# Query tiles of an attention in four places by turns, two of them shared with the quarters that the zs products load

## The chip, the cores and the metric

The kernel runs on one core of a Trainium2 chip. The core has five engines that run beside each other, each with an instruction queue of its own that is worked off in order: TensorE (PE, matrix products, with its weight loads shown apart as PEld), VectorE (DVE), ScalarE (ACT), GpSimd (POOL) and SyncE (SP, which here only issues DMAs). On-chip memory is divided into 128 partitions; matrix products land in eight banks of a second, smaller memory. The metric is the device time of one execution in microseconds.

## What is computed

One layer of a streaming encoder: x of 1024 tokens by 1024 channels, normalised, projected to queries, keys, values and five gates; a windowed attention (16 query heads, 2 key heads, 64 channels a head, keys of the own 64-token chunk and the two before it, one learned sink a head) and a spatial gating run side by side, are gated, projected, summed, projected again and added to x.

```python
proj = rmsnorm(x, norm_g) @ w_in
q, k, v, za, u, vs, zs, gm = jnp.split(proj, IN_SPLITS, axis=-1)
a = window_sink_attention(partial_rope(q), partial_rope(k), v, sinks)
a = (a * silu(za)) @ w_att_out
sgo = chunked_spatial_gating(gelu(u), gelu(vs), sg_w, sg_b, ln_g, ln_b)
sgo = (sgo * silu(zs)) @ w_sg_out
ga, gs = split(sigmoid(gm + b_merge))
x = x + (ga * a + gs * sgo) @ w_o
out = rmsnorm(x, final_g)
```

## The kernel before

Every float32 product is made of three products of rounded parts (a high and a low part of each factor), and every pair of 128-row weight blocks is multiplied in the manner of Strassen, with seven products of 12 matmuls instead of eight. `gemm_pair` (L327) does one pair: the products b11, t1, t2, b21, t3, b22 and t4 in this order, b11, t2, t3 and t4 adding onto one bank (`acc`), t1 and b22 onto another (`t5`), b21 into a third. ScalarE copies the bank after b11 into x11 (L336), after t1 into x22 (L340) and after t2 into x12 (L343); VectorE later adds to these tiles (L348, L353, L357), and each finished quarter goes to `finish`, the fourth in a further x tile. So a pair takes four x tiles, and the pool has five. Weights come through SP into `wr` tiles (L186), are split by ScalarE and VectorE (L151, L152), and the products read the parts.

After the products for q, the code runs four pairs for zs (m = 0, 2, 4, 6) through `zs_pair` (L936): the four quarters of a pair are kept in their x tiles, passed through Silu (L940), multiplied by quarters of the spatial gating's result (L943), which `get` loads from the scratch array s1_dr (L186), and stored to s_dr (L425). The profile shows both arrays as s_dr. For m = 0 the loaded quarters lie in the five `rot` places of an earlier pool; for m = 2, 4 and 6 in two places of the tag `g` in the pool `attention`. A quarter fills [128, 512] float32. Eight pairs for the gates gs and ga follow.

The attention runs beside the zs pairs of m = 2, 4, 6 and those of gs and ga. It has 32 steps: two key heads, eight token tiles of 128, two parities (which half of the query heads). `attention` (L1045) is a generator: in iteration n it emits the transposes of the weights of step n - 2 (L1015), then the scores and the softmax of step n (L975 to L1006), then the load of the query tile of step n + 2 (L923), then the product with the values of step n - 2 (L1034). `gemm_pair` calls a hook after each of its seven products, and each hook emits one or more of these parts: one in the zs pairs, 75/56 on average in the later ones. Seven hooks in the pair of m = 2 thus reach the scores of step 3, those of m = 4 the values of step 3 and the scores of step 5, those of m = 6 the scores of step 7 and the weights of step 6.

`query_stage` (L917) allocates the query tile, [128, 4, 128], which has the size of a quarter, and loads it with two DMAs; for every even step `key_stage` (L906) loads keys (L909) and values (L914) ahead of it. Query tiles have two places, tag `q` in the pool `ahead`, so that the tile of step n replaces that of step n - 2. `first_loads` issues those of steps 0 and 1 during the zs pair of m = 0.

The memory places are handed out when the instruction order is made, before the run: a tile that asks for a place of a tag gets one as soon as the last reader of a tile before it is listed, and its first writer then waits for that reader. The order on each engine's queue is listed in the same pass. It follows the order of the code where instructions are ready, and moves later ones ahead where earlier ones are not; on the chip each queue then keeps that order.

Of the kernel before, what the change touches and what calls it, by code (L numbers as in the profile page):

```python
# [25 lines left out]
F32R = mybir.dt.float32r  # L26
# [5 lines left out]
P = 128  # L32
# [22 lines left out]
def hybrid_tile(  # L55
# [25 lines left out]
    def nm(s):  # L81
        count[0] += 1
        return f"{s}_{count[0]}"
# [4 lines left out]
    def mtile(shape, dt, tag, bufs, pool=None):  # L88
        return (pool or main).tile(shape, dt, name=nm(tag), tag=tag, bufs=bufs)
# [621 lines left out]
    pool = stage.enter_context(tc.tile_pool(name="mixing", bufs=1))  # L711
# [90 lines left out]
    aheads = ahead.enter_context(tc.tile_pool(name="ahead", bufs=1))  # L802
    stage = ExitStack()
    pool = stage.enter_context(tc.tile_pool(name="queries", bufs=1))
# [94 lines left out]
    steps = [(g, t, par) for g in range(2) for t in range(NT) for par in range(2)]  # L899
# [5 lines left out]
    def key_stage(g, t):  # L905

        k0 = 0 if t else P
        kt = mtile([P, 2, 256], F32R, "k", 2, aheads)
        nc.sync.dma_start(  # L909
            kt[:, :, k0:].bitcast(F32), k_dr[:, 2 * g : 2 * g + 2, (t - 1) * P + k0 : (t + 1) * P]  # L910
        )
        vt = mtile([P, 2, 3 * HD], F32R, "v", 2, aheads)
        for j in key_tiles(t):
            nc.sync.dma_start(vt[:, j, :].bitcast(F32), v_dr[t - 1 + j, :, g, :])  # L914
        keys[g, t] = [kt, vt, None]

    def query_stage(g, t, par):  # L917
        if par == 0:
            key_stage(g, t)
        qt = mtile([P, 4, P], F32R, "q", 2, aheads)  # L920
        for j in range(2):
            rows = q_hl[j].rearrange("(c r d) t -> r d c t", r=2, d=HD)[par]
            nc.sync.dma_start(  # L923
                qt[j * HD : (j + 1) * HD].bitcast(F32), rows[:, 4 * g : 4 * g + 4, t * P : (t + 1) * P]
            )
        return qt
# [3 lines left out]
    def first_loads():  # L930
        for n in range(2):
            qT.append(query_stage(*steps[n]))
            yield
# [18 lines left out]
    pool = stage.enter_context(tc.tile_pool(name="attention", bufs=1))  # L952
# [92 lines left out]
    def attention():  # L1045

        held = []
        for n, step in enumerate(steps):
            if n >= 2:
                pT = weight_stage(*steps[n - 2], held.pop(0))  # L1050
                yield
            held.append(softmax_stage(*step, qT.pop(0)))
            if n + 2 < len(steps):
                qT.append(query_stage(*steps[n + 2]))
            yield
            if n >= 2:
                value_stage(*steps[n - 2], pT)
                yield
        for n in (-2, -1):
            pT = weight_stage(*steps[n], held.pop(0))  # L1060
            yield
            value_stage(*steps[n], pT)
            yield
# [25 lines left out]
    pool = stage.enter_context(tc.tile_pool(name="later", bufs=1))  # L1089
# [239 lines left out]
    for p in range(4):  # L1329
        n, t, acc, x11 = N_PAIRS + p, T_ORDER[p], accs[p], firsts[p]  # L1330
# [169 lines left out]
```

## Time and profile before

| | us |
|---|---|
| three runs | 965.46, 961.13, 967.64 |
| median | 965.46 |
| the profiled execution | 962.22 |
| its span, first to last instruction | 960.4 |
| TensorE without work in the span | 32.7 |
| the attention's scores, first to last | 328 to 630 |

The profile is of one execution. A row of the timeline gives the start, the length, the engine, the line, the operation and the names of what is written and read; in brackets stands how long the engine was idle before it and what ended that. A row of the waits gives who waited, for whom, how long in all, how often, and the longest. In the rows SPq is SP's queue of DMAs: its length is the time to issue, not to land.

### The profile page before, as it was taken

The page shows a single profiled execution, that of the slowest core. Times are in us where ns is not written, and L with a number is a line of the kernel's source. Part 1 is how long each engine was busy: PE and PEld are TensorE (multiplying, and loading weights), DVE is VectorE, ACT ScalarE, POOL GpSimd, SP SyncE. Part 2 cuts the span into 40 slices and gives each one's busy share as a digit, 9 for nine tenths or more (in the row PEclk, how much of TensorE's full clock was granted, in tenths as well). Part 3 has the DMA queues.
Part 4 walks back from the last instruction along what each step waited for, and adds up shares of the span by engine and source line. Part 5 has one row for each costly group of instructions (what it writes and reads, how often), then busy time and mean ns, then how long its engine had stood idle before and what let it go on. Part 6 is the DMA issues. An engine that isn't in the chain of part 4 may idle for free.

```text
span 960.4 us, 13432 instructions
## 1 busy us (share of the span) xinstructions
PE 927.7 (97%) x4452; PEld 767.6 (80%) x4452; DVE 692.0 (72%) x1321; ACT 558.1 (58%) x1061; POOL 120.5 (13%) x201
## 2 busy tenths in 40 slices
PE   6999999999999989999999998999999999999996
PEld 5888888888888878788878877888887887787885
DVE  6744677666675778788878876755589489569995
ACT  7864333333444489977767675754475465457443
POOL 0202212221000001211101111000110011210011
PEclk9999999999999999999999998999999999999999
DMA  7343767888669657876566694849758757979632
GB/s 277 121 128 129 212 211 187 184 156 191 214 231 319 201 184 209 228 197 158 156 210 218 210 229 122 215 145 321 287 197 309 286 191 246 272 190 306 219 122 87
DMA packets 126549, 198.64 MB, mean 207 GB/s; under 512 B 11408, under 2 KB 59280, under 8 KB 126480
## 3 DMA queue, kind: packets, MB, share of 16 engines
q1 hardware_dynamic: 108864, 149.28, 46.8%
q0 software_dynamic: 17472, 48.24, 21.2%
q8 instruction: 35, 0.57, 0.3%
q14 instruction: 34, 0.28, 0.1%
q10 hardware_dynamic: 144, 0.26, 0.1%
HBM read 141.65 MB, written 85.46 MB: 236 GB/s over the span
## 4 chain that ended last, share of the span: by engine, by line
PE 45%; DVE 9%; ACT 4%; DMA 3%; issue 3%; SPq 0%; DVEq 0%; ACTq 0%
PE ps_mm L318 19%; PE ps_o L318 15%; PE ps_sc L975 3%; PE ps_o L1034 3%; PE ps_tp L1015 2%; DMA wr<-in_w_dram 2%; DVE wl L152 2%; PE ps_tp L318 2%; PE ps_sc L318 2%; DVE bq L172 1%; DMA wr<-y_dr 1%; ACT pr L987 1%; ACT wh L151 1%; DMA g<-s_dr 0%; DVE T_t3l L152 0%
## 5 line engine op out<-in xcount | busy, mean ns | idle before, releaser
L151 ACT CAST wh<-s 128x1024 fp32r<-128x1024 f32 (+1 forms) x76 | 76.0, 1002 | 96.0 <-PE ps_mm L318 43.4
L151 ACT CAST wh<-wr 128x1024 fp32r<-128x1024 f32 (+1 forms) x78 | 64.5, 828 | 73.8 <-PE ps_mm L318 33.2
L152 DVE TENSOR_TENSOR wl<-wr,wh 128x1024 fp32r<-128x1024 f32 (+1 forms) x78 | 74.0, 950 | 43.7 <-ACT wh L151 42.8
L152 DVE TENSOR_TENSOR wl<-s,wh 128x1024 fp32r<-128x1024 f32 (+1 forms) x76 | 88.6, 1167 | 14.9 <-ACT wh L151 13.4
L987 ACT ACTIVATE pr<-pr,sm 128x256 f32<-128x256 f32 (+1 forms) x128 | 62.5, 490 | 23.6 <-DVE sm L977 23.3
L977 DVE CUSTOM_DVE_ANT_0 pr<-ps_sc,mask,nsink_sb 128x256 f32<-128x256 f32 (+1 forms) x128 | 56.3, 463 | 13.8 <-PE ps_sc L975 13.2
L318 PE MATMUL ps_o<-T_t1h,wh 128*128 128x512 f32 x144 | 57.3, 398 | 0.9 <-ACT wh L151 0.9
L318 PE MATMUL ps_o<-T_b22h,wh 128*128 128x512 f32 x144 | 57.2, 397 | 0.0
L318 PE MATMUL ps_mm<-T_b11h,wl 128*128 128x512 f32 x136 | 54.3, 399 | 2.4 <-DVE wl L152 2.4
L975 PEld LDWEIGHTS ps_sc<-k,q 128*128 128x128 f32 x256 | 40.4, 189 | 20.2 <-DVE sm L977 16.3
L318 PE MATMUL ps_o<-T_t1h,wl 128*128 128x512 f32 x144 | 56.3, 391 | 0.1
L975 PE MATMUL ps_sc<-k,q 128*128 128x256 f32 (+1 forms) x256 | 48.2, 294 | 8.5 <-DVE sm L977 8.4
L318 PE MATMUL ps_o<-T_b22h,wl 128*128 128x512 f32 x144 | 56.4, 392 | 0.0
L318 PE MATMUL ps_o<-T_b22l,wh 128*128 128x512 f32 x144 | 56.3, 391 | 0.0
L318 PE MATMUL ps_o<-T_t1l,wh 128*128 128x512 f32 x144 | 56.2, 390 | 0.0
L318 PE MATMUL ps_mm<-T_t4h,wh 128*128 128x512 f32 x136 | 54.1, 398 | 2.0 <-DVE x L353 2.0
L318 PE MATMUL ps_mm<-T_b11h,wh 128*128 128x512 f32 x136 | 54.9, 404 | 0.3 <-ACT wh L151 0.3
L318 PE MATMUL ps_mm<-T_b11l,wh 128*128 128x512 f32 x136 | 54.0, 397 | 0.0
L318 PE MATMUL ps_mm<-T_t3h,wh 128*128 128x512 f32 x136 | 53.7, 395 | 0.0
L318 PE MATMUL ps_mm<-T_t2h,wh 128*128 128x512 f32 x136 | 53.5, 393 | 0.1
L318 PE MATMUL ps_mm<-T_t4h,wl 128*128 128x512 f32 x136 | 53.2, 391 | 0.0
L318 PE MATMUL ps_mm<-T_t3h,wl 128*128 128x512 f32 x136 | 53.2, 391 | 0.0
(360 smaller groups left out, 2548.8 us busy)
## 6 DMA issues: line engine op xcount, KB each, us to landing
wr<-in_w_dram SPq DMA_DIRECT2D x82, 256.0 KB
sums<-in_w_dram POOLq DMA_DIRECT2D x20, 512.0 KB, 5.4
s<-sums SPq DMA_DIRECT2D x20, 512.0 KB
s_dr<-x SPq DMA_DIRECT2D x32, 256.0 KB
q_hl<-qhl SPq DMA_DIRECT2D x16, 512.0 KB
q<-q_hl SPq DMA_DIRECT2D x64, 128.0 KB
wr<-in_w_dram SPq DMA_DIRECT2D x14, 512.0 KB
y_dr<-x POOLq DMA_DIRECT2D x28, 256.0 KB, 5.5
```

Of the source, the lines that this page charges most:

```text
L151: nc.scalar.copy(hi, src)
L152: nc.vector.tensor_sub(lo, src, hi.bitcast(F32))
L172: op(dst[:, i : i + 2, :], a[:, i : i + 2, :], c[:, i : i + 2, :])
L318: nc.tensor.matmul(acc, lt, rt, start=fresh and k == 0 and n == 0, stop=k == 3 and n == 2, skip_group_check=True,)
L975: nc.tensor.matmul(sc[:, js], qt[:, i, :], kt[:, f, k0:], start=f == 0, stop=f == 1)
L977: nc.vector.tensor_tensor_reduce(pr[:, i, k0:], sc[:, js], mask[:, k0:], 1.0, nsink_sb[:, h : h + 1], op0=ALU.add, op1=ALU.min, accum_out= ...
L987: nc.scalar.activation(pr[:, i, k0:], pr[:, i, k0:], AF.Exp, bias=nmax[:, i : i + 1], scale=-1.0, accum_out=sums[:, i : i + 1],)
L1015: nc.tensor.transpose(pt[:, i * P : (i + 1) * P], pr[:, i, kt * P : (kt + 1) * P], ident[:])
L1034: nc.tensor.matmul(po[:], vv, parts[kt][:, n, :], start=kt == tiles[0] and n == 0, stop=kt == 1 and n == 1)
```

## The change

The query tiles of steps n with n % 4 equal to 0 or 1 keep the two places of the tag `q`. Those with n % 4 equal to 2 or 3 take the two places of the tag `g` in the pool that is open when the load is emitted, which is `attention`: the same two places that `zs_pair` uses for the quarters of s1_dr with m = 2, 4 and 6. Nothing else is changed; the loads, their sizes and the place in the code where they are emitted stay.

```diff
     def query_stage(g, t, par):
         if par == 0:
             key_stage(g, t)
-        qt = mtile([P, 4, P], F32R, "q", 2, aheads)
+
+        n = steps.index((g, t, par))
+        qt = mtile([P, 4, P], F32R, "q", 2, aheads) if n % 4 < 2 else mtile([P, 4, P], F32R, "g", 2, pool)
         for j in range(2):
             rows = q_hl[j].rearrange("(c r d) t -> r d c t", r=2, d=HD)[par]
             nc.sync.dma_start(
```

## The prediction

> **What bounds the kernel now.** First the page's busy times, then the table of stretches, cut where the attention runs beside the matrix products.
>
> ```profile
> span 960.4 us, 13432 instructions
> PE 927.7 (97%) x4452; PEld 767.6 (80%) x4452; DVE 692.0 (72%) x1321; ACT 558.1 (58%) x1061; POOL 120.5 (13%) x201
> ```
>
> ```profile
> 324.00:361.00 37.00, 34.24 (x166) 27.34 (x165) 27.76 (x70) 26.02 (x58) 0.60 (x3) 1.00 0.59 190
> 361.00:389.00 28.00, 26.60 (x135) 21.82 (x135) 24.47 (x66) 27.68 (x58) 4.14 (x5) 1.00 0.74 200
> 389.00:412.00 23.00, 23.00 (x116) 19.38 (x117) 18.25 (x42) 22.32 (x45) 4.14 (x5) 1.00 0.88 232
> 570.00:600.00 30.00, 25.80 (x123) 20.99 (x122) 17.93 (x47) 16.67 (x42) 3.99 (x5) 0.89 0.58 160
> ```
>
> The columns are length, then PE, PEld, DVE, ACT and POOL busy, the granted clock, the DMA share and GB/s. TensorE bounds the kernel: it idles for 960.4 - 927.7 = 32.7 us in all. In the three stretches from 324 to 412, where the zs pairs of m = 2, 4 and 6 run with the first eight steps of the attention, it idles for 2.76, 1.40 and 0 us, and ScalarE is as full: 27.68 of 28 and 22.32 of 23 us. So in the two later ones a wait on ScalarE is nearly as dear as one on TensorE.
>
> Next, who waits for a query tile. The first fence is from the answer for the tile q, the second from SP's own waits.
>
> ```profile
> L923 SPq DMA_DIRECT2D q<-q_hl x64: 573/592/727, 299.6 to 613.3; - x64
> its engine sat idle before it (us, times) until:
>   DVE sm L977: 24.7, 29
> ```
>
> ```profile
> SPq L923 <- PE ps_sc L975: 52.1, 25, 4.7
> ```
>
> The score matmuls sat idle for 24.7 us, and each time until VectorE had read a score bank (L977); no load of q ended such a wait. SP stood 52.1 us at L923 until the scores that read the old tile were done, but nobody waited for what it then loaded. The rows of SP in time show the margin, and date the steps: in this stretch each load of a q tile starts when the scores two steps earlier end.
>
> ```profile
> 329.99 1.03 SPq L425 DMA_DIRECT2D s_dr<-x  x2
> ...
> 339.61 0.38 SPq L186 DMA_DIRECT2D g<-s_dr  x1
> ...
> 354.43 1.24 SPq L923 DMA_DIRECT2D q<-q_hl  x2
> ...
> 362.45 1.24 SPq L923 DMA_DIRECT2D q<-q_hl  x2
> ...
> 365.39 1.92 SPq L186 DMA_DIRECT2D g<-s_dr  x2
> ...
> 381.14 1.24 SPq L923 DMA_DIRECT2D q<-q_hl  x2
> ...
> 389.41 1.24 SPq L923 DMA_DIRECT2D q<-q_hl  x2
> ...
> 400.62 1.24 SPq L923 DMA_DIRECT2D q<-q_hl  x2
> ```
>
> These q rows are the loads for steps 4, 5, 7, 8 and 9 (tile n waits for step n - 2), so the scores of step 2 end at 354.43, of step 3 at 362.45, of step 6 at 389.41 and of step 7 at 400.62. The tile of step 7 starts loading at 381.14 and is first read at 393.67 (row below): 12.5 us of margin.
>
> **The change part by part.**
>
> *Four places for q.* Tiles of steps 2, 3, 6, 7, 10, 11 and so on move to the g places; the others keep the two q places. A tile now replaces the one of four steps earlier, so it can be loaded about two steps sooner. No instruction or byte is added. The gain is 0: no score matmul waited for q. SP's stand isn't removed with certainty either: a load is listed as soon as its place is free, and then SP stands for the scores that free it, as before. What a better SP order could give is bounded by TensorE's idle time in the rows above: 2.76 + 1.40, plus the one wait at 579 us and the low clock behind it (below), 4.20 + 2.0, together 10.4 us. I take 0, as the row for q says.
>
> *Steps 0 to 3.* The two g places are requested in the order of the code: tiles of steps 2 and 3 first, then the four quarters A, B, C, D that the zs pair of m = 2 loads from s1_dr (its products' x11, x22, x12 and the fourth). Before, both places were free for quarters: A of m = 2 was loaded at 339.61. Now A has to wait for the scores of step 2.
>
> *Steps 6 and 7.* These hold both g places when the quarters of m = 4 ask: A of m = 4, loaded at 365.39 so far, cannot start before the scores of step 6 end, at 389.41. For m = 6 nothing holds a place except earlier quarters and step 7.
>
> *Who waits for a late quarter.* VectorE multiplies it into an x tile (L943), SP stores that (L425), and only then is the x tile free. There are five x places and each pair takes four, so x22 of the next pair (L340) takes the place of A, and x12 (L343) that of B. The price of one quarter, from rows:
>
> ```profile
> 344.35 0.69 DVE L943 TENSOR_TENSOR x<-x,g 128x512 f32<-128x512 f32 x1 [2.48 <-DMA g<-s_dr]
> ```
>
> ```profile
> 335.55 0.60 ACT L340 ACTIVATE x<-ps_o 128x512 f32<-128x512 f32 x1 [5.46 <-DMA s_dr<-x]
> ...
> 361.30 0.60 ACT L340 ACTIVATE x<-ps_o 128x512 f32<-128x512 f32 x1
> ...
> 367.18 0.58 ACT L343 COPY x<-ps_mm 128x512 f32<-128x512 f32 x1
> ...
> 389.65 0.62 ACT L340 ACTIVATE x<-ps_o 128x512 f32<-128x512 f32 x1
> ...
> 393.67 0.56 ACT L343 COPY x<-ps_mm 128x512 f32<-128x512 f32 x1
> ```
>
> ```profile
> 339.61 4.64 DMA g<-s_dr
> ...
> 407.64 2.77 PE ps_mm L318 x12
> ```
>
> Load 4.64, multiply 0.69, store until the place is free 335.55 - 329.99 = 5.5: 10.8 us from a free g place to a free x place. The last fence, from the chain of waits, also gives one product of 12 matmuls, 2.77.
>
> Join of m = 2 and 4: A starts at 354.43, so x22 is free at 365.2, against 361.30 before: 3.9 late. B starts on the same place when A is multiplied, 354.43 + 4.64 + 0.69 = 359.8 (the other place comes free only at 362.45), so x12 is free at 370.6, against 367.18: 3.4 late. Join of m = 4 and 6: A starts at 389.41, x22 is free at 400.2 against 389.65, 10.6 late; B starts at 394.7, x12 is free at 405.5 against 393.67, 11.9 late. (Should x12, which is named first in the code, take A's place and x22 that of B, the later of the two is free at the same time.)
>
> *What hides it.* The product t3 adds onto the bank that x12's copy must have read first; b22 in the same way needs x22's copy. Neither needs the other, and b21 needs none.
>
> ```profile
> 382.79 1.03 PE L1015 MATMUL ps_tp<-ident,pr 128*128 128x128 f32 x8
> ...
> 386.43 0.63 PE L975 MATMUL ps_sc<-k,q 128*128 128x256 f32 x4
> 388.47 0.91 PE L975 MATMUL ps_sc<-k,q 128*128 128x256 f32 x4 [1.40 <-DVE sm L977]
> ...
> 391.95 1.10 PE L1034 MATMUL ps_o<-pT,v 128*128 128x512 f32 x4
> ...
> 393.67 0.72 PE L975 MATMUL ps_sc<-k,q 128*128 128x256 f32 x4
> ...
> 394.46 0.39 PE L318 MATMUL ps_mm<-T_t3h,wh 128*128 128x512 f32 x1
> ...
> 397.21 0.40 PE L318 MATMUL ps_o<-T_b21h,wh 128*128 128x512 f32 x1
> ```
>
> At 4 to 6, t3 started at 394.46, right after x12's copy, and b21 after it. With x12 late by 11.9, b21 can go ahead (2.77), then b22 once x22 is copied (2.77), then one step of the attention: 1.03 + 1.10 + 2 x 0.63 = 3.4. That leaves 11.9 - 8.9 = 3.0 us of idle TensorE. Below it is bounded by 0 (more work of the next pair or step pulled ahead), above by 11.9 (nothing pulled ahead). At 2 to 4, b22 alone hides 2.77 of 3.4, leaving 0.6; but x22's copy stands 3.9 us on ScalarE, with the exponentials and the splits of the weights queued behind it, and ScalarE is busy 27.68 of 28 us there: bounds 0.6 and 3.9. I take 2.5, nearer the upper end, since the row at 335.55 shows that copy standing 5.46 us in front of ScalarE's queue rather than being moved behind other work. VectorE's multiplies are in-order too, with the score reads behind them; the row at 344.35 has such a stand of 2.48, and it is inside these bounds.
>
> Sum: 0 + 2.5 + 3.0 = 5.5 us. Against the profiled run (span 960.4, run 962.22) that makes 967.7. The runs shown have the median 965.46, which is 3.2 above the profiled one; on that scale the forecast is 971.0.
>
> A longer idle time has a second price here:
>
> ```profile
> 579.52 0.79 PE L975 MATMUL ps_sc<-k,q 128*128 128x256 f32 x2 [4.20 <-DVE sm L977]
> ```
>
> ```profile
> 569.52 8.76 DMA wr<-in_w_dram
> 581.16 4.79 PE ps_mm L318 x12
> ```
>
> After 4.20 us of idle the next product took 4.79 instead of 2.77, 2.0 us more, and the stretch 570 to 600 has a granted clock of 0.89; after the 1.40 at 388.47 the clock stayed 1.00. [...]
>
> **The rivals.**
>
> *All covered.* The order of the work is listed before the run; if more of the attention or of the next pair's b11 is pulled into the gap, nothing is left: 0 us, 965.5. For it: TensorE was full from 389 to 412 with no gap. Against it: ScalarE, equally full, has no room for what is pulled ahead.
>
> *Not slower, faster.* The one long wait that a better SP order could shorten is at 569.52: the load of weights stands there behind the loads of v on SP and lands 8.76 us later. If q loads taken earlier clear SP by then and the lists change so that it goes a few us sooner, the 4.20 and the 2.0 go: -6.2, with the joins covered 959.3. It decides from the point where this load starts 4.2 us earlier. Against it: the loads of v, not q, stand right before it, and they stay.
>
> *Uncovered.* If the lists reckon the loads shorter than they are, the late copies sit in ScalarE's queue in front of work that TensorE needs: 3.9 + 11.9 + 2.0 for the clock = 17.8, 983.3. For it: both stands of that kind in the rows above (5.46 on ScalarE, 2.48 on VectorE).
>
> **How the numbers follow.** Forecast 0.45, all covered 0.17, faster 0.12, uncovered 0.26. The range 960 to 983 runs from the faster case to the uncovered one and leaves about half of each outside. One per cent, about what a measurement of this kernel can tell from no change, is 9.65 us. Slower by more: most of the uncovered case (0.24) and the upper part of the forecast (0.10), 0.34. Faster by more would take nearly the whole bound of 10.4: 0.04. Within: 0.62.
>
> **What would show it.** In the changed profile: loads of quarters of m = 4 no earlier than the scores of step 6 (L975), against 365.39; waits of L340 and L343 for s_dr<-x or for L943 of 3 us and more between 355 and 410; idle TensorE of 5 to 6 us more from 324 to 412 and none less behind it. The number of score waits put down to VectorE should stay near 29. The prediction is wrong if quarters get a place before the tiles of steps 6 and 7, if score matmuls turn out to wait for q loads, or if the time changes outside that stretch.

## The result, and the profile after

| | median, us | runs |
|---|---|---|
| before | 965.46 | 7, 961.13 to 969.67 |
| changed | 974.03 | 7, 972.74 to 975.66 |

The ratio is 1.0093 with a 95% interval of 1.0071 to 1.0115; by the medians the change is 8.6 us slower. The profiled execution of the changed kernel took 975.66 us, the longest of its seven runs, and that of before took 962.22, near the shortest of its own; so the two traces differ by 13.4 us, more than the medians do.

Where the difference arises is read off one copy that every pair makes, ScalarE's of the first product into x11 (L336). Its starts in the two timelines:

| pair | before, us | changed, us | difference |
|---|---|---|---|
| zs, m = 2 | 329.51 | 330.59 | +1.1 |
| zs, m = 4 | 360.11 | 358.71 | -1.4 |
| zs, m = 6 | 388.23 | 390.46 | +2.2 |
| first gate pair | 411.44 | 417.54 | +6.1 |
| second gate pair | 438.62 | 449.05 | +10.4 |
| a late pair | 797.11 | 807.75 | +10.6 |
| the last but one shown | 838.80 | 851.96 | +13.2 |

From 439 to 797 us nothing is added. The last 2.6 us appear at a wait for weights, and the traces of two kernels measured as fast as before (e1 and e3 below) show 2.1 and 3.1 us more there as well, so they are not put down to the change. The first 2.5 us are a gain, and then three joins cost 3.6, 3.9 and 4.3 us. These are differences of one trace each: between the same copies, up to the second gate pair, e1 is up to 1.7 us longer than before and e3 up to 2.8, without any measured loss, so a single join is known no better than that.

The same stretches as before from the table by stretches of the changed kernel (length, PE, PEld, DVE, ACT and POOL busy, granted clock, DMA share, GB/s):

```profile
324.00:361.00 37.00, 36.04 (x176) 29.14 (x176) 28.59 (x76) 28.09 (x61) 0.60 (x3) 1.00 0.55 168
361.00:389.00 28.00, 25.11 (x125) 20.12 (x123) 21.99 (x57) 24.31 (x51) 3.66 (x5) 1.00 0.82 204
389.00:412.00 23.00, 21.14 (x100) 16.89 (x101) 15.17 (x41) 19.07 (x41) 3.87 (x5) 1.00 0.69 178
412.00:435.00 23.00, 18.69 (x82) 13.86 (x82) 16.70 (x40) 16.26 (x36) 3.30 (x4) 0.93 0.78 199
```

and the last of them before:

```profile
412.00:435.00 23.00, 23.00 (x120) 18.84 (x119) 19.81 (x54) 16.84 (x43) 3.29 (x4) 1.00 0.85 214
```

TensorE's idle time over the four stretches is 0.96 + 2.89 + 1.86 + 4.31 = 10.0 us, against 2.76 + 1.40 + 0 + 0 = 4.2 before; the largest part is in the last stretch, behind the zs pairs, where VectorE and ScalarE are less busy as well. The timeline of SP shows what came late, the loads of quarters (g from s_dr) and the stores behind their multiplication:

```profile
390.74 0.33 SPq L186 DMA_DIRECT2D g<-s_dr  x1
394.78 0.33 SPq L425 DMA_DIRECT2D s_dr<-x  x1
395.20 0.38 SPq L186 DMA_DIRECT2D g<-s_dr  x1
399.18 0.32 SPq L425 DMA_DIRECT2D s_dr<-x  x1
399.59 0.38 SPq L186 DMA_DIRECT2D g<-s_dr  x1
402.99 0.32 SPq L425 DMA_DIRECT2D s_dr<-x  x1
403.36 0.42 SPq L186 DMA_DIRECT2D g<-s_dr  x1
...
406.86 0.58 SPq L186 DMA_DIRECT2D g<-s_dr  x1
...
411.44 0.55 SPq L186 DMA_DIRECT2D g<-s_dr  x1
...
416.08 0.38 SPq L186 DMA_DIRECT2D g<-s_dr  x1
...
424.12 0.46 SPq L186 DMA_DIRECT2D g<-s_dr  x1
```

These are the four quarters of m = 4 and the four of m = 6. Before, the first load of m = 4 was issued at 365.39; now it is at 390.74, and the four of m = 4 go one by one, each behind the multiplication of the one before it, while the tile of step 7 holds the other place. That place comes free when the scores of step 7 end at 405.8, and the first quarter of m = 6 takes it at 406.86. The chain of waits of the changed kernel goes through the first quarter of m = 4, from the scores of step 6 to the product that had to wait for x22:

```profile
389.80 0.92 PE ps_sc L977 x4
390.74 3.30 DMA g<-s_dr
394.06 0.69 DVE x L945
394.78 2.27 DMA s_dr<-x
397.07 0.61 ACT x L340
397.72 4.88 PE ps_o L318 x19
```

The scores are L977 now and the multiplication L945, as the change adds two lines. At the third join the chain goes through the first quarter of m = 6, which is multiplied only 8.06 us after its load was issued, to a split of weights (L152) behind that multiplication:

```profile
406.86 8.06 DMA g<-s_dr
...
415.55 1.22 DVE wl L152
```

Why this load took so much longer than the 3.30 us of the other is not shown. Where the late loads are paid for is in the waits between 338 and 450 us; first of the changed kernel, then of before (who waited, for whom, us in all, times, longest):

```profile
DVE x L945 <- DMA g<-s_dr: 14.7, 9, 3.1
```

```profile
DVE x L943 <- DMA g<-s_dr: 5.4, 4, 2.5
```

VectorE stands 14.7 us instead of 5.4 in front of a multiplication whose quarter has not landed, with everything listed behind it. The stand for the first quarter of m = 6, in VectorE's and then TensorE's timeline:

```profile
414.94 0.69 DVE L945 TENSOR_TENSOR x<-x,g 128x512 f32<-128x512 f32 x1 [3.06 <-DMA g<-s_dr]
415.55 1.22 DVE L152 TENSOR_TENSOR wl<-s,wh 128x1024 fp32r<-128x1024 f32 x1
```

```profile
416.83 0.50 PE L318 MATMUL ps_o<-T_t1h,wl 128*128 128x512 f32 x1 [1.84 <-DVE wl L152]
...
418.27 0.63 PE L318 MATMUL ps_o<-T_t1l,wh 128*128 128x512 f32 x1
```

The split of weights (L152) sits behind a multiplication with which it has nothing to do, and the product t1 of the first gate pair waits 1.84 us for it; it then runs at half the clock for some 3.4 us (0.50 in each stretch of 1 us from 418 to 421), which costs up to 1.7 us more (an estimate: the missing share of the granted clock, added up over the stretches of 1 us from 417 to 422).

### The profile page after: what moved, and what is told of

Same layout as the page of the kernel before. It is cut to its first block, busy times and chain, and to the rows that moved or that the text cites. A ratio compares the mean times of both kernels' runs of the same rounds, so it can differ in the third digit from the quotient of the medians.

```text
span 973.9 us, 13426 instructions
## 1 busy us (share of the span) xinstructions
PE 932.6 (96%) x4452; PEld 768.9 (79%) x4452; DVE 691.6 (71%) x1321; ACT 559.7 (57%) x1061; POOL 122.3 (13%) x201
## 4 chain that ended last, share of the span: by engine, by line
PE 70%; DVE 12%; DMA 11%; issue 4%; ACT 2%; SPq 1%; DVEq 0%; ACTq 0%
PE ps_mm L318 27%; PE ps_o L318 20%; PE ps_mm L575 5%; DMA wr<-in_w_dram 3%; DVE wl L152 3%; PE ps_sc L977 3%; DMA g<-s_dr 3%; PE ps_o L1036 2%; PE ps_tp L1017 2%; PE ps_o L528 2%; PE ps_sc L318 2%; PE ps_tp L318 2%; PE ps_tp L762 1%; DMA wr<-in_x_dram 1%; DVE bq L172 1%
## 5 line engine op out<-in xcount | busy, mean ns | idle before, releaser
L152 DVE TENSOR_TENSOR wl<-wr,wh 128x1024 fp32r<-128x1024 f32 (+1 forms) x78 | 73.9, 947 | 45.5 <-ACT wh L151 44.8
L152 DVE TENSOR_TENSOR wl<-s,wh 128x1024 fp32r<-128x1024 f32 (+1 forms) x76 | 88.4, 1164 | 13.8 <-ACT wh L151 13.0
L979 DVE CUSTOM_DVE_ANT_0 pr<-ps_sc,mask,nsink_sb 128x256 f32<-128x256 f32 (+1 forms) x128 | 56.1, 462 | 12.7 <-PE ps_sc L977 12.3
L318 PE MATMUL ps_mm<-T_t4l,wh 128*128 128x512 f32 x136 | 53.6, 394 | 0.0
L318 PE MATMUL ps_mm<-T_t3l,wh 128*128 128x512 f32 x136 | 53.1, 390 | 0.0
```

Of the source, the lines that this page charges most:

```text
L152: nc.vector.tensor_sub(lo, src, hi.bitcast(F32))
L318: nc.tensor.matmul(acc, lt, rt, start=fresh and k == 0 and n == 0, stop=k == 3 and n == 2, skip_group_check=True,)
L979: nc.vector.tensor_tensor_reduce(pr[:, i, k0:], sc[:, js], mask[:, k0:], 1.0, nsink_sb[:, h : h + 1], op0=ALU.add, op1=ALU.min, accum_out= ...
```

## The experiments

Two theories go in. The first is the prediction's: query tiles of steps 2, 3, 6 and 7 keep the quarters out of the g places. The second: four places as such, with loads taken sooner and a new order of the work, cost the time. Each run has a ratio to runs of the kernel before on the same chip; the time differences are that ratio less 1, times 965.46.

**e1. Sharing from step 10 on.**

```diff
-        qt = ... if n % 4 < 2 else mtile([P, 4, P], F32R, "g", 2, pool)
+        qt = ... if n % 4 < 2 or n < 8 else mtile([P, 4, P], F32R, "g", 2, pool)
```

> Steps 2, 3, 6 and 7 go back to the two q places; from step 10 on the tiles take the g places, as in the changed kernel. Theory (tiles of steps 2, 3, 6, 7 keep the quarters of m = 2, 4, 6 out of the g places, so x tiles come free late): the loss of 8.6 us goes, the time is that of before within 2 us. Rival (loads taken two steps sooner disturb SP's order or the DMAs all through the attention): 24 of the 32 steps still have four places, so most of the loss stays, 5 us and more over before.

Measured 0.9996 (0.9965 to 1.0027): the time of before. The sharing from step 10 on costs nothing, although most tiles still have four places. The second theory is out as far as those steps go.

**e2. Steps 6 and 7 alone.**

```diff
-        qt = ... if n % 4 < 2 else ...
+        qt = ... if n not in (6, 7) else ...
```

> Only the tiles of steps 6 and 7 lie in g places, all others in the two q places. Theory: the joins of m = 4 with 6 and of m = 6 with the first gate pair still cost 3.9 and 4.3 us, the join of m = 2 with 4 nothing: 6 to 9 us over before. Rival (four places as such): only 2 of 32 tiles have moved, so within 2 us of before.

Measured 1.0051 (1.0026 to 1.0077), 4.9 us: less than the 6 to 9 expected, and clear of the other theory's 2 us. In its trace the copies L336 fall 4.3 and 3.8 us further behind those of before at the two joins, 388 to 411 and 411 to 439, and VectorE stands 14.8 us for quarters.

**e3. Steps 2 and 3 alone.**

```diff
-        qt = ... if n % 4 < 2 else ...
+        qt = ... if n not in (2, 3) else ...
```

> Only the tiles of steps 2 and 3 lie in g places. Theory: the join of m = 2 with 4 costs some 3.5 us, but the first quarter of m = 2 no longer makes VectorE stand at 344 us, which gave back some 2 us in the trace of the changed kernel: 0 to 4 us over before. Rival (four places as such): within 2 us of before, with no change at the join.

Measured 0.9981 (0.9952 to 1.0009), no loss and no gain clear of noise. The join of m = 2 and 4 is there in the trace (from -1.4 to +1.4 us), and so is the gain ahead of it: VectorE stands 2.7 us for quarters, half as long as before. The trace is 4.2 us late at 411, with no query tile in the way of m = 4 or 6: TensorE waited 1.74 us at 389.84 for VectorE's read of a score bank, where before it waited 1.40, and here the clock was at half for some 3.4 us behind it. By 439 it is 2.8 us late.

**e4. Quarters ask first.** The first two quarters of a pair get their tiles, and their loads, in front of the pair's products in the code.

```diff
         quarters = []
+        first = [get(s1_dr, m + i, half, *place) for i, half in ((0, 0), (1, 1))] if m else []
         gemm_pair(hb, lambda *quarter: quarters.append(quarter), hook)
...
-            g = get(s1_dr, m + i, half, *place)
+            g = first.pop(0) if first else get(s1_dr, m + i, half, *place)
```

> The changed kernel, with the first two quarters of m = 2, 4 and 6 requested ahead of the pair's products in the code, so that they get the g places before the query tiles of steps 2, 3, 6, 7. Nothing else is moved. Theory: the first two quarters of m = 4 load near 365 us again and the x tiles come free in time; the time is that of before within 3 us. Rival (four places as such): it stays 8 us over before. Third way: the scores now wait for query tiles that come late, 3 us and more over before with score waits ended by a DMA.

Measured 1.0090 (1.0060 to 1.0119), 8.7 us, which misses the expectation and has the size that the theory of four places as such gave; e1 and e12 speak against that theory. SP's timeline says what happened:

```profile
364.59 0.32 SPq L186 DMA_DIRECT2D g<-s_dr  x1
...
365.85 0.38 SPq L186 DMA_DIRECT2D g<-s_dr  x1
...
369.32 0.48 SPq L186 DMA_DIRECT2D g<-s_dr  x1
...
391.79 0.33 SPq L186 DMA_DIRECT2D g<-s_dr  x1
```

The first is the last quarter of m = 2; the next two, the first quarters of m = 4, load at 365.85 and 369.32 as wished, but the third only at 391.79 (before, at 374.12), because the tiles of steps 6 and 7 now follow the first two in the places. VectorE's stands are 12.3 us. No score matmul waited for a DMA, so the third way of the expectation didn't come either. Asking first moves the first two quarters and leaves the other six late.

**e5 and e6. No quarters.** Loads of and multiplications by the quarters of m = 2, 4 and 6 are left out, in the kernel before (e5) and in the changed one (e6).

```diff
         for i, half, q, src, sign in quarters:
-            g = get(s1_dr, m + i, half, *place)
-            nc.vector.tensor_mul(q[:], q[:], g[:])
+            if m == 0:
+                g = get(s1_dr, m + i, half, *place)
+                nc.vector.tensor_mul(q[:], q[:], g[:])
             put(s_dr, m + i, half, q[:])
```

> The kernel before, with the loads of quarters of s1_dr and the multiplications by them left out for m = 2, 4 and 6 (s_dr then holds the Silu of zs alone for these rows). It is the baseline for the next run. Theory: some 2 us under before, since VectorE no longer stands for the first quarter at 344 us; the rival has no other number.

> The changed kernel with the same left out, so that the query tiles have four places and share them with nobody. Theory: within 2 us of the kernel before with the same left out, or a little faster. Rival (four places as such cost): 5 us and more slower than that.

Measured 0.9970 (0.9946 to 0.9995), 2.9 us under before, and 0.9981 (0.9956 to 1.0007). With nobody to share with, four query places are neither slower nor faster than two within these intervals: the change's loss is the sharing, and its gain, with the sharing taken away, is not measurable.

**e7 and e8. Step 6 alone, step 7 alone.**

```diff
-        qt = ... if n % 4 < 2 else ...
+        qt = ... if n != 6 else ...        (e8: n != 7)
```

> Only the tile of step 6 lies in a g place. Theory: one place stays for the quarters of m = 4, so the first loads near 370 us, the others follow one by one on it: 0 to 3 us over before, less than half of what steps 6 and 7 together cost. If instead the loss grows with the number of tiles moved, it is half of that of steps 6 and 7.

> Only the tile of step 7 lies in a g place. Theory: as for step 6 alone, but the place is held until the scores of step 7 end, near 400 us, so that the quarters of m = 6 begin on one place as well: 1 to 4 us over before.

Measured 1.0073 (1.0041 to 1.0106), 7.0 us, and 1.0048 (1.0023 to 1.0072), 4.6 us. Both miss: within the intervals one tile costs as much as two (e2). In e7 nothing is lost up to the first gate pair (+0.5 us at 411), then 4.9 us up to 439, and 3.8 more between 466 and 495. The 4.9 us go with a single stand of VectorE, for the last quarter of m = 6: TensorE waits 3.21 us behind it, and the clock is at half for some 3.4 us after that (0.50 from 425 to 427). The stand in e7 and then in e8:

```profile
422.14 0.69 DVE L945 TENSOR_TENSOR x<-x,g 128x512 f32<-128x512 f32 x1 [4.48 <-DMA g<-s_dr]
```

```profile
423.20 0.69 DVE L945 TENSOR_TENSOR x<-x,g 128x512 f32<-128x512 f32 x1 [4.50 <-DMA g<-s_dr]
```

That load was issued at 415.70 in e7 and 416.80 in e8, hardly later than before (414.70), but took 6.4 us to the multiplication in both, where before took 3.6. Why it took longer stays open. The 3.8 us behind 466, where no quarter is left, are two waits of TensorE, 1.06 us at 473.43 and 0.84 at 475.23, for a split on VectorE (L152), and half the clock for some 3.4 us from 475.5. In the chain of waits they go back to a load of weights, 8.02 us from 458.77, and a load of keys of 2.60 us behind it; whether the moved tile had a part in that stays open.

**e9 and e10. Multiplications on GpSimd**, in the kernel before (e9) and the changed one (e10).

```diff
-            nc.vector.tensor_mul(q[:], q[:], g[:])
+            if m:
+                nc.gpsimd.tensor_tensor(q[:], q[:], g[:], op=ALU.mult)
+            else:
+                nc.vector.tensor_mul(q[:], q[:], g[:])
```

> The kernel before, with the multiplications by the quarters of m = 2, 4 and 6 on GpSimd instead of VectorE. Theory (the price is VectorE standing in front of a multiplication whose quarter has not landed): before stands 5.4 us there in all, so 0 to 4 us under before. Rival: GpSimd's own queue, with the paced sums in it, releases the x tiles late, and it is 3 us and more over before.

> The changed kernel with the same move. Theory (VectorE's stands, 14.7 us in the trace of the changed kernel): over the run before it by less than 4 us, half of the 8.6 us. Rival (x tiles come free late, whichever engine multiplies): still 6 us and more over the run before it.

Measured 0.9992 (0.9966 to 1.0018) and 1.0160 (1.0131 to 1.0188): the changed kernel is 15.4 us over, nearly double its loss and far from the theory's 4 us. So the price isn't bound to VectorE. But the run doesn't single out the x tiles either, since the stand moved on to two other queues. From the waits and then SP's timeline of e10:

```profile
POOL x L946 <- DMA g<-s_dr: 32.4, 6, 15.8
...
DVE s L222 <- DMA wr<-in_w_dram: 10.7, 2, 5.6
```

```profile
410.25 2.04 SPq L914 DMA_DIRECT2D v<-v_dr  x2
417.00 0.32 SPq L425 DMA_DIRECT2D s_dr<-x  x1
417.37 0.93 SPq L186 DMA_DIRECT2D g<-s_dr  x2
```

GpSimd stands 32.4 us for quarters, SP stands from 412.3 to 417.00 for a product to store, with the next loads of quarters queued behind the store, and TensorE has a wait of 6.3 us that ends at 424.83. The clock is at half for some 6.8 us at that wait (0.50 from 423 to 427), and at another of 4.7 us that ends at 390.61 as well.

**e11. The changed kernel without the quarters of m = 6.** Their loads and multiplications are left out.

```diff
-            g = get(s1_dr, m + i, half, *place)
-            nc.vector.tensor_mul(q[:], q[:], g[:])
+            if m < 6:
+                g = get(s1_dr, m + i, half, *place)
+                nc.vector.tensor_mul(q[:], q[:], g[:])
```

> The changed kernel with loads and multiplications by the quarters left out for m = 6 alone (those rows of s_dr hold the Silu of zs alone). Theory: the 4.3 us lost between the first gate pair's start and 440 us go, what is lost at the two joins before stays: 2 to 6 us over before. Rival (what is lost at 390 us only moves on to 440 us): 7 us and more over before, or none.

Measured 1.0071 (1.0045 to 1.0097), 6.9 us, between the two numbers. By the trace, the third join (411 to 439) loses 1.5 us instead of 4.3, and what is lost before it stays (+5.9 at 411). So in the traces the quarters of m = 6 carry some 2.8 us of the third join. That is as much as a join differs between traces without any loss, and the difference between the 6.9 us and the change's own loss lies within the intervals; so the share of each join isn't settled by this run.

**e12. All but steps 6 and 7.**

```diff
-        qt = ... if n % 4 < 2 else ...
+        qt = ... if n % 4 < 2 or n in (6, 7) else ...
```

> The changed kernel with the tiles of steps 6 and 7 alone back in the two q places; steps 2, 3, 10, 11 and so on stay in g places. Theory (the loss is what steps 6 and 7 do to the quarters of m = 4 and 6): the whole loss goes, within 3 us of before, 0 to 3 us under it if the early loads of steps 2 and 3 give back what they gave at 344 us. Rival (no one tile decides, any new order of the work costs): 4 us and more over before.

Measured 1.0000 (0.9976 to 1.0024). With two of the 32 tiles taken back, the whole loss is gone. No version that does all of the work beats the kernel before by more than its interval.

VectorE's stands for quarters between 338 and 450 us, as in the waits above, separate the kernels that multiply on VectorE with all quarters kept, and so does the granted clock in the stretch from 412 to 435:

| kernel | stands, us | clock, 412 to 435 | ratio |
|---|---|---|---|
| e12 | 2.4 | 1.00 | 1.0000 |
| e3 | 2.7 | 1.00 | 0.9981 |
| before | 5.4 | 1.00 | 1 |
| e1 | 6.2 | 1.00 | 0.9996 |
| e7 | 10.5 | 0.93 | 1.0073 |
| e4 | 12.3 | 0.93 | 1.0090 |
| e8 | 12.3 | 0.93 | 1.0048 |
| changed | 14.7 | 0.93 | 1.0093 |
| e2 | 14.8 | 0.93 | 1.0051 |

Up to 6.2 us they cost nothing that can be measured, from 10.5 on some 5 to 9 us; within these groups the order isn't kept. In every slower kernel the clock fell to half once in that stretch, behind a wait for VectorE of 1.7 to 3.3 us, which by the table makes up at most some 0.07 x 23 = 1.6 us of the loss (an estimate). The fall comes with the stand, so the two aren't told apart here. e11, without the quarters of m = 6, stood 7.7 us, had 0.93 there as well, and cost 6.9 us.

## Why the prediction was right, point by point

The forecast of 971.0 was 3 us short of 974.03: the direction and the mechanism were right, one join was left out. That the sum came so near is in part luck: the delays were taken too long and the cover too large, and the third join and the early gain, both missing from the sum, have opposite signs.

- *Four places bring nothing.* Right: e6 against e5, and e1 and e12. No score matmul waited for a load, and the early 2.5 us that the trace did gain had another source, not foreseen: VectorE no longer stood 2.48 us at 344 us for the first quarter of m = 2, since that quarter now loads at 353.04. The gain recurs in the traces of e3 and e12 (2.1 and 2.4 us), but doesn't show in their times beyond the intervals.
- *Tiles ask for the places before the quarters.* Right: the first quarter of m = 4 goes at 390.74, 0.02 us after the scores of step 6 end at 389.80 + 0.92; e12 shows that steps 6 and 7 are what costs.
- *10.8 us from a free g place to a free x place.* Too long: 390.74 to 397.07 is 6.3 us, 3.30 for the load and 2.27 for the store, where 4.64 and 5.5 were taken from single rows of before; a load's time isn't one number, since that of the first quarter of m = 6 took 8.06. So x22 and x12 of m = 6 came at 397.07 and 401.88, 7.4 and 8.2 late, not 10.6 and 11.9; those of m = 4 at 364.99 and 369.01, 3.7 and 1.8 late, where 3.9 and 3.4 were said.
- *What hides it.* The products b22 and b21 were pulled ahead of t3 as said, b22 first. The cost left over was 3.6 us (said 2.5) at the first join and 3.9 us (said 3.0) at the second, from smaller delays and less cover: the copies stood 0.69 us at most, as the listed order had already put them late, and the standing was on VectorE instead.
- *The step that failed:* "For m = 6 nothing holds a place except earlier quarters and step 7." That is true, and its price was taken as nothing. Step 7's scores run to 405.8 in the changed kernel, so the four quarters of m = 4 share one place in turn, the first of m = 6 is loaded at 406.86 instead of 390.70, the last is multiplied at 429.21 instead of 418.30, and the third join costs 4.3 us in the trace, up to 1.7 of them by the clock. In the trace of e11 2.8 of them are gone.
- *The signs to look for.* Idle TensorE of 5 to 6 us more came true for the stretch up to 435 (5.9), but only 1.6 of it lies before 412, where all of it should have been. The waits of L340 and L343 for s_dr<-x didn't come at 3 us or more: they were 0.69 at most; of the multiplication's waits one between 355 and 410 came near (2.36). The score matmuls waited for VectorE 34 times instead of 29, 30.1 us instead of 24.7. And one of the prediction's own signs of being wrong, a time that changes outside 324 to 412, came true for the third join.
- *The clock.* The forecast's sum holds waits of up to 3.0 us and no price for the clock; it fell after 1.84 (below), and a second price was paid where none was reckoned.
- *The rivals.* All covered and faster are out. Uncovered, 17.8 us, had the right form (queues standing in order) and was placed at the wrong engine: VectorE stood, not ScalarE, and 8.6 us came of it. In e10, where the stand was moved to GpSimd, the loss was 15.4 us.

What stays open: how much of each join is x tiles that come free late, and how much VectorE's stand. Every run changed both. The clock's part is an estimate, and no run took it away alone.

## What to carry to other kernels

Before two streams share places, list who asks for each place in time order, and how long each holds it: here two tiles, loaded at 368 and 372 us and first read at 388 and 391, left four short-lived quarters one place in turn and made the next four late, for a prefetch that nobody had waited for. Here a load that became late was paid for on the queue of whoever read it (14.7 us of stands on VectorE, 32.4 on GpSimd in e10), by work behind the reader that had nothing to do with it (the split of weights, for which TensorE waited 1.84 us). Follow the shared place through to the last user, not only to the first join.

## What the runs showed of the hardware that had not been expected

The granted clock fell after a wait of only 1.84 us. In the changed kernel's fine table of stretches (columns as above):

```profile
415.00:417.00 2.00, 0.17 (x1) 0.18 (x2) 1.97 (x3) 1.97 (x3) 0.00 (x0) 1.00 0.60 219
417.00:419.00 2.00, 2.00 (x7) 1.61 (x8) 1.97 (x3) 1.12 (x3) 0.82 (x1) 0.72 0.48 170
419.00:421.00 2.00, 2.00 (x5) 1.02 (x4) 1.97 (x4) 0.35 (x1) 0.00 (x0) 0.50 0.43 131
421.00:423.00 2.00, 1.24 (x5) 0.72 (x5) 2.00 (x5) 0.24 (x1) 0.84 (x1) 0.92 0.03 8
423.00:425.00 2.00, 2.00 (x11) 1.39 (x10) 2.00 (x7) 1.90 (x3) 0.00 (x0) 1.00 0.83 130
```

The clock was still full for the first matmuls behind the wait, and at half speed from 417.9 to some 421.3: the rows of single matmuls start 0.43 us apart there instead of 0.23. Before, the waits of 1.57 us that ended at 346.10 and of 1.40 that ended at 388.47 were followed by a clock of 1.00, and the one of 4.20 that ended at 579.52 by 0.50 from 579 to 585. The length of the wait alone doesn't decide: in e12 the clock stayed at 1.00 after 1.83 us (at 391.24), and in e1 it fell to 0.50 after 1.47 (at 346.29), at a wait that in the kernel before took 1.57 and left it at 1.00. What else decides isn't shown here. Each fall between 324 and 512 us in the traces of the changed kernel, e1, e2, e3, e4, e7, e8 and e11 lasted 3.4 us at half the clock, after waits of 0.84 to 3.25 us, and so cost up to 1.7 us (an estimate, as above); the two of e10 lasted 6.8.
